# Up projections of both MLPs as pair products, with the halves of the bank added as it is emptied

## The chip, the cores and the metric

The kernel runs on one core of a Trainium2 chip. Its time is the device time of one execution in microseconds; before and after are compared by the median of several executions on the same chip. A profiled execution is recorded as well: every instruction of each engine with its start and duration.

The engines are TensorE (PE in the profile, with its weight loads as PEld), VectorE (DVE), ScalarE (ACT), GpSimd (POOL) and SyncE (SP, which here only issues DMAs). TensorE writes its products into eight banks of 512 float32 columns in each of 128 partitions.

## The reference

A decoder trunk of two layers over a sequence of 256 tokens with 1024 features. The first layer mixes tokens with a gated linear recurrence, the second with sparse attention; behind each mixer stands a squared-ReLU MLP, and the change is in the MLPs alone:

```python
def _sq_relu_mlp(h, w_up, w_down):
    u = jax.nn.relu(h @ w_up)
    return (u * u) @ w_down

def reference(x, ...):
    for i in range(DEPTH):
        h = _rmsnorm(x, norm_mix[i])
        ...
        h = _rmsnorm(x, norm_ffn[i])
        x = x + _sq_relu_mlp(h, mlp_w_up[i], mlp_w_down[i])
    return _rmsnorm(x, norm_final)
```

All inputs are float32. `w_up` is 1024 x 4096 and `w_down` 4096 x 1024, so the up projection of an MLP has 32 chunks of 128 output features.

## The kernel before

**Products in parts.** To come close to float32 with the faster format float32r, each operand is split into a rounded part (high) and the rest (low). A product of weights w and input x is then wh·xh + wh·xl + wl·xh. Two helpers issue this for one step, that is one block of 128 input features:

- `mm3` (L373 to L377) makes three products of 256 columns each, all into the same 256 columns of a bank.
- `mm2` (L379 to L382), the pair, makes two. The first has 512 columns: wh times the high and the low part of x, which lie side by side; it fills both halves of the bank. The second, of 256 columns, adds wl·xh to the lower half. The two halves have to be added later.

**The MLP** (`mlp`, from L832) runs twice. Its input is the tile `hhl` (L549), which holds for each of the KC = 8 feature blocks the high and the low part, 256 columns each, side by side (`hh` and `hl` are views of it). In the up projection a chunk m of 128 output features takes 8 steps, from one weight piece of 128 x 1024. The first chunks (`first`; LEADS = 3 in the first MLP, 4 in the second) have been issued by the section before. The others use `mm3` on the lower half of the next bank from `zrot`, a rotation over six banks. After each chunk `up_post` empties the bank:

- VectorE takes the maximum with 0 and multiplies by `rs`, the factor of the norm (L843), into `t`.
- `flush()` issues what was put off by the chunk before: the low part of the squares (L850).
- `tick` (L344) prepares coming weight pieces: `split_lo` (VectorE, L331) makes the low part of a piece whose high part exists, and `split_hi` (ScalarE, L322) rounds the next one, both only while fewer than LOOK = 6 pieces are ahead. A DMA on SP's queue fills one of NRAW = 5 raw buffers, four pieces ahead of `split_hi`; the split pieces lie in NSPL = 7 pairs of buffers.
- ScalarE squares `t` twice, into `u` in float32 (L848) and rounded into `uh` (L849).

The down projection has 8 chunks of 32 steps. Chunks 0 to 6 use `mm2` on the tiles `uhl`, and chunk 7 uses `mm3`. At the end of a pair chunk ScalarE copies the upper half of the bank into `part` (L876), `residual` adds the lower half to `xt` (L595), and VectorE adds `part` (L879).

Each engine works through its queue in the program's order. In the MLPs that order is the order of the lines; in the sections before them (recurrence, attention and the lead-in chunks) it is worked out when the program is built, by a list scheduler with assumed durations, and is the same in every execution.

Of the kernel before, what the change touches and what calls it, by code (L numbers as in the profile page):

```python
# [12 lines left out]
F32 = mybir.dt.float32  # L13
F32R = mybir.dt.float32r
AF = mybir.ActivationFunctionType
OP = mybir.AluOpType
# [3 lines left out]
P = 128  # L20
S = 256
D = 1024
KC = D // P
# [249 lines left out]
def trunk_kernel(ctx: ExitStack, tc: tile.TileContext, x_in, vec_in, const_in, w2_in, wts, out):  # L273
    nc = tc.nc
    ctx.enter_context(tc.manual_schedule())
    pe, dve, act, pool = nc.tensor, nc.vector, nc.scalar, nc.gpsimd
# [12 lines left out]
    def rotation(*ids):  # L289
        while True:  # L290
            for i in ids:
                yield bank(i)
# [22 lines left out]
    def split_hi(eng=None):  # L315
        i = state["split"]
        if i >= len(order):
            return
        while state["dma"] <= min(i + 4, len(order) - 1):
            issue()  # L320
        n = piece_cols(*order[i])
        (act.copy if eng is None else eng.tensor_copy)(hi_t[i % NSPL][:, :n], raw_t[i % NRAW][:, :n])  # L322
        state["split"] += 1

    def split_lo(eng=None):
        i = state["lo"]
        if i >= state["split"]:
            return
        n = piece_cols(*order[i])
        hi, lo = hi_t[i % NSPL], lo_t[i % NSPL]  # L330
        (eng or dve).tensor_tensor(lo[:, :n], raw_t[i % NRAW][:, :n], hi[:, :n].bitcast(F32), op=OP.subtract)  # L331
        state["lo"] += 1
# [3 lines left out]
    def later(fn):  # L336
        deferred.append(fn)

    def flush():
        todo, deferred[:] = deferred[:], []  # L340
        for fn in todo:
            fn()

    def tick(lo=None, hi=None, n=1):  # L344
        for i in range(max(n, 1)):
            more = n and state["split"] - state["get"] < LOOK
            if more:
                split_lo(lo)
            if i == 0:
                flush()  # L350
            if more:
                split_hi(hi)

    def get(name, idx):
        i = state["get"]
        assert order[i] == (name, idx), (order[i], name, idx)
        state["get"] += 1
        assert state["lo"] > i
        return hi_t[i % NSPL], lo_t[i % NSPL]

    def turn(x):
        return x.rearrange("p (a b) -> p b a", a=2)

    def pairs(z):
        return z.rearrange("p (b a) -> p b a", a=2)

    def nat(z):
        return z.rearrange("p (b a) -> p a b", a=2)

    def two(x):  # L370
        return x.rearrange("p (a b) -> p a b", a=2)

    def mm3(ps, wh, wl, xh, xl, start, stop):  # L373
        ps, xh, xl = pairs(ps), turn(xh), turn(xl)
        pe.matmul(ps, wh, xh, start=start, stop=False)  # L375
        pe.matmul(ps, wh, xl, start=False, stop=False)  # L376
        pe.matmul(ps, wl, xh, start=False, stop=stop)  # L377

    def mm2(z, wh, wl, x, start, stop):  # L379
        xd = x.rearrange("p (i a b) -> p i b a", i=2, a=2)  # L380
        pe.matmul(z.rearrange("p (i b a) -> p i b a", i=2, a=2), wh, xd, start=start, stop=False)  # L381
        pe.matmul(pairs(z[:, :S]), wl, xd[:, 0], start=False, stop=stop)  # L382
# [166 lines left out]
    hhl = hpool.tile([P, KC, 2, S], F32R, name="hhl")  # L549
    hh, hl = hhl[:, :, 0], hhl[:, :, 1]  # L550
    acc = spool.tile([P, S], F32, name="acc")
    rs = spool.tile([P, S], F32, name="rstd")
# [41 lines left out]
    def residual(z, m):  # L594
        dve.tensor_tensor(two(xt[:, m]), two(xt[:, m]), nat(z), op=OP.add)  # L595


    with ExitStack() as ph:
# [41 lines left out]
        for k in range(KC):  # L640
            g = vec[:, V_GM + k:V_GM + k + 1]
            t = 0.6 * k - 3
# [4 lines left out]
                w=[("hh", k)], t=t)  # L647
# [3 lines left out]
        for q in range(4):  # L651
            for i in range(NFINE):
                w = slice(256 * q, 256 * q + 256)
                hi, lo, rw = hi_t[i][:, w], lo_t[i][:, w], raw_t[i][:, w]
                rk = [("raw0", i, q), ("raw", i)]
                t = 1.2 * q + 0.3 * i - 2.9
                add([("dve", 0.2, 0.0), ("act", 0.31, 0.5)], copy(hi, rw), r=rk, w=[("hi0", i, q)], t=t)
                add("dve", 0.34, diff(lo, rw, hi), r=rk + [("hi0", i, q)], w=[("lo0", i, q)],
                    t=t + 0.1)
        for a, b, n in ((0, 2, 2), (0, 1, 1), (4, 6, 2), (4, 5, 1), (0, 4, 1)):  # L660
            add("dve", 0.07 + 0.267 * n, lambda e, a=a, b=b, n=n: e.tensor_tensor(
                x2[:, a:a + n], x2[:, a:a + n], x2[:, b:b + n], op=OP.add), r=[("x2", b + i) for i in range(n)],
                w=[("x2", a + i) for i in range(n)], t=4 + a / 4)
# [44 lines left out]
        def nextbank():  # L708
            zb["n"] += 1
            return (0, 1, 2, 3, 4, 5, 7)[(zb["n"] - 1) % 7]  # L710
# [105 lines left out]
        for m in range(8):  # L816
            wh, wl, wk = sec.weight("out", m, to + 2.65 * m)
            b = nextbank()
            z = sec.bank(("out", m), b, zcols)
# [6 lines left out]
            t = to + 2.65 * (m + 1)  # L826
# [5 lines left out]
    def mlp(layer, epilogue, first, late=None):  # L832
        with ExitStack() as ph:
            up = ph.enter_context(tc.tile_pool(name="up%d" % layer, bufs=1, side="right"))
            tmp = ph.enter_context(tc.tile_pool(name="mtmp%d" % layer, bufs=2))
            uhl = [up.tile([P, 2 * S], F32R, name="uhl", tag="uhl", bufs=NF) for _ in range(NF)]
            uh, ul = [x[:, :S] for x in uhl], [x[:, S:] for x in uhl]
            zrot = rotation(*((LEADS[layer] + i) % 6 for i in range(6)))
            part = [tmp.tile([P, S], F32, name="part", tag="part", bufs=1)]

            def up_post(m, z):
                t = tmp.tile([P, S], F32, name="t", tag="t")
                dve.scalar_tensor_tensor(two(t), nat(z), 0.0, two(rs), op0=OP.max, op1=OP.mult)  # L843
                flush()
                if m >= len(first) - 1:
                    tick(n=2 if m < 16 else 1)
                u = tmp.tile([P, S], F32, name="u", tag="u")
                act.activation(u, t, AF.Square)  # L848
                act.activation(uh[m], t, AF.Square)  # L849
                later(lambda: dve.tensor_tensor(ul[m], u, uh[m].bitcast(F32), op=OP.subtract))  # L850

            for m in range(NF):
                if m >= len(first):
                    z = next(zrot)[:, :S]
                    wh, wl = get("up%d" % layer, m)
                    for k in range(KC):
                        w = slice(k * P, (k + 1) * P)
                        mm3(z, wh[:, w], wl[:, w], hh[:, k], hl[:, k], k == 0, k == KC - 1)
                else:
                    z = first[m]()  # L860
                up_post(m, z)
            for m in range(8):
                z = next(zrot)
                for j in range(4):
                    if j == 3 and late and m == 7:
                        late()
                    wh, wl = get("dn%d" % layer, m * 4 + j)
                    for k in range(8):
                        w, i = slice(k * P, (k + 1) * P), j * 8 + k
                        if m < 7:  # L870
                            mm2(z, wh[:, w], wl[:, w], uhl[i], i == 0, i == NF - 1)
                        else:
                            mm3(z[:, :S], wh[:, w], wl[:, w], uh[i], ul[i], i == 0, i == NF - 1)
                    if j == 3:
                        if m < 7:
                            act.copy(two(part[0]), nat(z[:, S:]))  # L876
                        residual(z[:, :S], m)
                        if m < 7:
                            dve.tensor_tensor(xt[:, m], xt[:, m], part[0], op=OP.add)  # L879
                        epilogue(m)  # L880
                    tick()
# [4 lines left out]

    nc.gpsimd.dma_start(w2raw, w2_in)
    mlp(0, to_mix, up0)


    with ExitStack() as ph:
# [108 lines left out]
        for i in range(2):  # L1000
            pecol = (V_PEK, V_PEV)[i]
            add("pool", 0.15, lambda e, i=i, c=pecol: e.tensor_copy(zf[:, ZW * i + 60], vec[:, c:c + 16]), r=zok + ["vec"],
                w=[("z", i, "p")], t=-5)
# [304 lines left out]
        def out_t(half, m, b, t, step):  # L1308
            wh, wl, wk = weight("o%d" % half, m // 2, t)
            z = zview(("out", half, m), b, zcols)  # L1310
            for ks in ((0, 1), (2, 3)) if half == 0 else ((0, 1), (2,), (3,)):
                def run(e, ks=ks):
                    for kk in ks:
                        o = (m % 2) * 512 + kk * P
                        k = half * 4 + kk
                        mm3(z(), wh[:, o:o + P], wl[:, o:o + P], oh(k), ol(k), kk == 0, kk == 3)
                add("pe", 0.355 * len(ks), run, r=wk + [(n, half * 4 + kk) for n in ("oh", "ol") for kk in ks],
                    w=[("ps", b)], t=t)
                t += step * len(ks) / 2
            add("dve", 0.34, lambda e: residual(z(), m), r=[("ps", b)], w=[("xt", m)], t=t)  # L1320
            return t
# [14 lines left out]
        t, tp_, nb, early = 0.0, {}, 0, True  # L1336
        for x in PROJ:
# [15 lines left out]
            if x == AFTER:  # L1353
                t = max(t, tc_ + TQ)
# [27 lines left out]
        for m in range(8):  # L1382
            t = out_t(1, m, (2, 3, 4, 0, 1)[m % 5], te - 2 + 1.4 * m, PJ)
# [10 lines left out]

    st = bank(6)
    mlp(1, to_final, up1, lambda: square_sums(st, acc, True, False))
    square_sums(st, sqs[1], False, True)
    act.activation(rcol, st[:, :2], AF.Sqrt, bias=epst, scale=1.0 / D)
# [120 lines left out]
```

## Time and profile before

| | us |
|---|---|
| timed executions | 569.47, 569.96, 570.29 (median 569.96) |
| profiled execution | 569.74 |
| its span, first to last instruction | 567.9 |

The span in stages, read from where the lines of each stage start and end: the recurrence and its projections up to about 87 us, the first MLP from there to about 258 us (down projection from 174), attention to about 387 us, the second MLP to about 559 us (down projection from 474), and the last norm. A row of the view of groups names line, engine, operation, output and inputs with their shapes, then the busy time, the mean of one in ns, and the idle time before them with what ended it. A row of the timeline gives start, duration, engine, line and operation, and in brackets the idle time of the engine before it and who ended that. The durations of products overlap, because TensorE takes the next one while the last is still flowing out; the pace is read from the starts.

### The profile page before, as it was taken

What the parts mean: (1) busy time and instruction counts of PE and PEld (TensorE: products, weight loads), DVE (VectorE), ACT (ScalarE), POOL (GpSimd) and SP (SyncE); (2) the same over time, 40 slices, a digit from 0 to 9 for tenths busy, and PEclk for the clock granted to TensorE, in tenths of its full rate; (3) what the DMA queues carried; (4) which work ended last, traced back from release to release, by engine and by line L of the source; (5) the groups of instructions that cost most, each with busy time, mean ns of one, the idle gap of its engine ahead of it and who ended that gap; (6) DMA issues with size and microseconds to landing.
All of it is one profiled execution on the core that took longest, in us unless ns stands there. A gap on an engine that the chain in (4) does not pass through costs nothing.

```text
span 567.9 us, 11331 instructions
## 1 busy us (share of the span) xinstructions
PE 553.5 (97%) x4318; PEld 531.4 (94%) x4318; DVE 429.3 (76%) x884; ACT 370.2 (65%) x738; POOL 51.1 (9%) x63
## 2 busy tenths in 40 slices
PE   8999999999999999999999999998999999999994
PEld 8999999999999999999998997988999999999994
DVE  5999999776775674767999999899876776465532
ACT  6699775766664543546899899996865665354420
POOL 0310000000000211312000101000000000142220
PEclk9999999999999999999999999999999999999997
DMA  8935465655566466566745464542765566556402
GB/s 272 404 139 186 149 221 207 228 199 187 194 211 228 154 216 219 172 189 247 227 149 165 105 171 118 149 94 89 268 217 191 193 209 216 198 176 214 167 1 74
DMA packets 32614, 105.25 MB, mean 185 GB/s; under 512 B 3984, under 2 KB 6944, under 8 KB 32560
## 3 DMA queue, kind: packets, MB, share of 16 engines
q1 hardware_dynamic: 30784, 99.70, 52.5%
q0 software_dynamic: 1200, 4.29, 3.4%
q8 instruction: 34, 0.56, 0.4%
q10 hardware_dynamic: 576, 0.53, 0.3%
q14 instruction: 20, 0.16, 0.1%
HBM read 101.36 MB, written 1.05 MB: 180 GB/s over the span
## 4 chain that ended last, share of the span: by engine, by line
PE 77%; ACT 10%; DVE 8%; issue 2%; DMA 1%; SPq 1%; DVEq 0%; ACTq 0%
PE bank L381 17%; PE bank L375 15%; PE bank L376 15%; PE bank L377 15%; PE bank L382 9%; PE bank L752 2%; ACT pt L1233 2%; ACT pt L1252 2%; ACT whl L388 2%; ACT pth L1266 1%; DMA raw<-in_dram 1%; DVE whl L385 1%; DVE pt L1230 1%; ACT zwoh L388 1%; ACT osum L1299 1%
## 5 line engine op out<-in xcount | busy, mean ns | idle before, releaser
L375 PE MATMUL bank<-hhl,whl 128*128 128x256 f32 x768 | 213.7, 278 | 0.4 <-ACT hhl L643 0.4
L376 PE MATMUL bank<-hhl,whl 128*128 128x256 f32 x768 | 211.5, 275 | 0.1
L377 PE MATMUL bank<-hhl,whl 128*128 128x256 f32 x768 | 211.5, 275 | 0.1
L331 DVE TENSOR_TENSOR whl<-raw,whl 128x1024 fp32r<-128x1024 f32 x117 | 146.0, 1269 | 2.8 <-ACT whl L322 2.8
L375 PEld LDWEIGHTS bank<-hhl,whl 128*128 128x128 f32 x768 | 147.0, 191 | 1.0 <-ACT hhl L643 0.6
L376 PEld LDWEIGHTS bank<-hhl,whl 128*128 128x128 f32 x768 | 147.0, 191 | 0.8 <-DVE hhl L645 0.5
L377 PEld LDWEIGHTS bank<-hhl,whl 128*128 128x128 f32 x768 | 147.0, 191 | 0.4 <-DVE whl L385 0.3
L381 PE MATMUL bank<-uhl,whl 128*128 128x512 f32 x448 | 146.8, 382 | 0.0
L322 ACT CAST whl<-raw 128x1024 fp32r<-128x1024 f32 (+1 forms) x118 | 119.9, 1039 | 9.9 <-ACT whl L322 5.6
L382 PE MATMUL bank<-uhl,whl 128*128 128x256 f32 x448 | 122.1, 273 | 0.0
L381 PEld LDWEIGHTS bank<-uhl,whl 128*128 128x128 f32 x448 | 84.7, 189 | 11.8
L382 PEld LDWEIGHTS bank<-uhl,whl 128*128 128x128 f32 x448 | 86.0, 192 | 0.0
L385 DVE TENSOR_TENSOR whl<-raw,whl 128x1024 fp32r<-128x1024 f32 (+3 forms) x69 | 72.6, 1072 | 0.6 <-ACT whl L388 0.4
L595 DVE TENSOR_TENSOR xt<-xt,bank 128x256 f32<-128x256 f32 x40 | 16.1, 415 | 72.0 <-ACT part L876 58.5
L388 ACT CAST whl<-raw 128x1024 fp32r<-128x1024 f32 (+2 forms) x64 | 60.0, 959 | 6.0 <-DMA raw<-in_dram 4.3
L848 ACT ACTIVATE u<-t 128x256 f32<-128x256 f32 x64 | 26.7, 416 | 53.8 <-DVE t L843 52.5
L843 DVE SCALAR_TENSOR_TENSOR t<-bank,rstd 128x256 f32<-128x256 f32 x64 | 26.9, 423 | 41.5 <-PE bank L377 40.5
L876 ACT COPY part<-bank 128x256 f32<-128x256 f32 x14 | 5.2, 372 | 61.8 <-PE bank L382 61.8
L1233 ACT ACTIVATE pt<-pt,mx 128x128 f32<-128x128 f32 (+1 forms) x64 | 28.6, 450 | 2.1 <-DVE mx L1230 2.1
L850 DVE TENSOR_TENSOR uhl<-u,uhl 128x256 fp32r<-128x256 f32 x64 | 26.6, 416 | 1.8 <-ACT uhl L849 1.7
L565 POOL TENSOR_TENSOR acc<-xt 128x256 f32<-128x256 f32 x2 | 2.9, 1460 | 265.3 <-issue 152.4
L565 POOL TENSOR_TENSOR sq<-xt 128x256 f32<-128x256 f32 x12 | 17.3, 1442 | 94.6 <-DVE xt L879 86.5
(214 smaller groups left out, 871.2 us busy)
## 6 DMA issues: line engine op xcount, KB each, us to landing
raw<-in_dram SPq DMA_DIRECT2D x171, 512.0 KB, 4.4
whl<-in_dram POOLq DMA_DIRECT2D x8, 512.0 KB, 5.7
gw<-in_dram SPq DMA_DIRECT2D x4, 512.0 KB, 9.4
raw<-in_dram SPq DMA_DIRECT2D x5, 256.0 KB, 6.4
xt<-in_dram SPq DMA_DIRECT2D x4, 256.0 KB, 5.6
zwol<-in_dram SPq DMA_DIRECT2D x2, 512.0 KB, 5.4
raw<-in_dram SPq DMA_DIRECT2D x2, 456.0 KB, 3.9
kh<-th SPq DMA_DIRECT2D x8, 64.0 KB, 3.4
```

Source lines behind the costliest of these rows:

```text
L322: (act.copy if eng is None else eng.tensor_copy)(hi_t[i % NSPL][:, :n], raw_t[i % NRAW][:, :n])
L331: (eng or dve).tensor_tensor(lo[:, :n], raw_t[i % NRAW][:, :n], hi[:, :n].bitcast(F32), op=OP.subtract)
L375: pe.matmul(ps, wh, xh, start=start, stop=False)
L376: pe.matmul(ps, wh, xl, start=False, stop=False)
L377: pe.matmul(ps, wl, xh, start=False, stop=stop)
L381: pe.matmul(z.rearrange("p (i b a) -> p i b a", i=2, a=2), wh, xd, start=start, stop=False)
L382: pe.matmul(pairs(z[:, :S]), wl, xd[:, 0], start=False, stop=stop)
L385: return lambda e: e.tensor_tensor(o, a, h.bitcast(F32), op=OP.subtract)
L388: return lambda e: (e.copy if e is act else e.tensor_copy)(o, a)
L843: dve.scalar_tensor_tensor(two(t), nat(z), 0.0, two(rs), op0=OP.max, op1=OP.mult)
L848: act.activation(u, t, AF.Square)
L1233: add("act", (0.39, 0.49)[qc], lambda e, row=row, j=j: e.activation(row, row, AF.Exp, bias=mx[:, j:j + 1], scale=-1.0, accum_out=sm[:, j:j ...
```

## The change

The chunks of the up projections that the MLP issues itself now use `mm2` on the whole bank. In `up_post` such a chunk has ScalarE copy the upper half of the bank into a new tile `b`, then comes the tick (which also flushes), and only then VectorE adds the lower half and `b` into `t` and takes the maximum and the factor in place. The lead-in chunks, which another function issues with `mm3`, are emptied as before.

```diff
             def up_post(m, z):
                 t = tmp.tile([P, S], F32, name="t", tag="t")
-                dve.scalar_tensor_tensor(two(t), nat(z), 0.0, two(rs), op0=OP.max, op1=OP.mult)
-                flush()
+                if m < len(first):
+                    dve.scalar_tensor_tensor(two(t), nat(z), 0.0, two(rs), op0=OP.max, op1=OP.mult)
+                    flush()
+                else:
+                    b = tmp.tile([P, S], F32, name="b", tag="b")
+                    act.copy(two(b), nat(z[:, S:]))
                 if m >= len(first) - 1:
                     tick(n=2 if m < 16 else 1)
+                if m >= len(first):
+                    dve.tensor_tensor(two(t), nat(z[:, :S]), two(b), op=OP.add)
+                    dve.scalar_tensor_tensor(t, t, 0.0, rs, op0=OP.max, op1=OP.mult)
                 u = tmp.tile([P, S], F32, name="u", tag="u")
                 act.activation(u, t, AF.Square)
                 act.activation(uh[m], t, AF.Square)
@@
                 if m >= len(first):
-                    z = next(zrot)[:, :S]
+                    z = next(zrot)
                     wh, wl = get("up%d" % layer, m)
                     for k in range(KC):
                         w = slice(k * P, (k + 1) * P)
-                        mm3(z, wh[:, w], wl[:, w], hh[:, k], hl[:, k], k == 0, k == KC - 1)
+                        mm2(z, wh[:, w], wl[:, w], hhl[:, k].rearrange("p i s -> p (i s)"), k == 0, k == KC - 1)
                 else:
                     z = first[m]()
                 up_post(m, z)
```

## The prediction

> **What bounds the kernel now.** I read the page's table of busy shares and its chain first, because they say which engine the end hangs on.
>
> ```profile
> PE 553.5 (97%) x4318; PEld 531.4 (94%) x4318; DVE 429.3 (76%) x884; ACT 370.2 (65%) x738; POOL 51.1 (9%) x63
> PEclk9999999999999999999999999999999999999997
> PE bank L381 17%; PE bank L375 15%; PE bank L376 15%; PE bank L377 15%; PE bank L382 9%; PE bank L752 2%; ACT pt L1233 2%; ACT pt L1252 2%; ACT whl L388 2%; ACT pth L1266 1%; DMA raw<-in_dram 1%; DVE whl L385 1%; DVE pt L1230 1%; ACT zwoh L388 1%; ACT osum L1299 1%
> ```
>
> TensorE is busy 97% of the span at a granted clock that is full almost throughout, and the chain lies mostly on the products of mm3 (L375 to L377) and mm2 (L381, L382). A busy share of pipelined products doesn't say that they run back to back, so I asked for the stretch in which the change acts (the windows view): 24 chunks of the first up projection, then all pair chunks of the down projection behind it, then its last chunk, which still uses mm3.
>
> ```profile
> 107.03:171.35 64.32, 64.32 (x578) 64.32 (x577) 45.45 (x72) 40.01 (x72) 0.00 (x0) 1.00 0.59 197
> 173.83:247.19 73.36, 73.36 (x450) 67.42 (x449) 45.20 (x49) 32.40 (x41) 13.02 (x11) 1.00 0.61 205
> 247.19:257.91 10.72, 10.72 (x98) 10.72 (x97) 6.68 (x7) 4.67 (x6) 2.32 (x2) 1.00 0.56 183
> ```
>
> The columns are length, PE, PEld, DVE, ACT, POOL, granted clock, DMA share, GB/s. PE has no idle time in any of the three, the clock is 1.00, and in the up stretch VectorE works 45.45 of 64.32 us and ScalarE 40.01. So the pace of the up projections is the pace at which TensorE takes products, and the other engines have about 0.78 us (VectorE) and 1.01 us (ScalarE) of slack in each of the 24 chunks.
>
> **What a step of each form costs.** The ends of these stretches come from the timeline.
>
> ```profile
> 107.03 0.42 DVE L843 SCALAR_TENSOR_TENSOR t<-bank,rstd 128x256 f32<-128x256 f32 x1 [0.79 <-PE bank L377]
> 171.35 0.42 DVE L843 SCALAR_TENSOR_TENSOR t<-bank,rstd 128x256 f32<-128x256 f32 x1 [0.79 <-PE bank L377]
> 173.83 0.38 PE L381 MATMUL bank<-uhl,whl 128*128 128x512 f32 x1
> 174.05 0.27 PE L382 MATMUL bank<-uhl,whl 128*128 128x256 f32 x1
> 174.16 0.38 PE L381 MATMUL bank<-uhl,whl 128*128 128x512 f32 x1
> 247.19 0.28 PE L375 MATMUL bank<-uhl,whl 128*128 128x256 f32 x1
> 257.91 0.28 PE L375 MATMUL bank<-hhl,whl 128*128 128x256 f32 x1
> ```
>
> L843 empties a bank as soon as its chunk is done, so its starts tick with the chunks: 25 of them from 107.03 to 171.35 make 24 chunks in 64.32 us, 2.680 us a chunk and, with 8 steps, **335.0 ns a step of mm3**. The down projection holds 7 chunks of 32 pair steps between 173.83 and 247.19: 73.36 / 224 = **327.5 ns a step of mm2**. Its eighth chunk, on the same input tiles, with mm3, takes 10.72 / 32 = 335.0 ns. Both forms stream 768 columns a step, so the pair saves nothing in columns; it saves one product and one weight load of three, and that is worth 7.5 ns. The eighth chunk is the check that the form is the cause and not the stage.
>
> **Part 1, the products.** The change gives the pair form to 32 - 3 = 29 chunks of the first MLP and 32 - 4 = 28 of the second; the lead-in chunks keep mm3. 57 x 8 = 456 steps x 7.5 ns = **3.42 us** off TensorE. The trace doesn't show a pair with hhl as moving operand. Its bounds are 335.0 ns (nothing gained) and 327.5 ns; I take 327.5, the nearest row, since the width, the weights, the bank rotation and the layout (high part, then low part, in 512 adjacent columns) are those of L381.
>
> That sum can be put beside a rule. The fixed cost per product in these rows: with c for 256 columns and f for a start, 3c + 3f = 335.0 and 3c + 2f = 327.5, so f = 7.5 ns.
>
> The Trainium skill, page "TensorE: Matmul & The Clock Gate", section "Back-to-back issue gap", gives a product of N columns a time of N / 2.4 + 2.5 ns at full clock. By that rule a step would save 2.5 ns and the change an estimated 1.14 us. The trace doesn't agree with it in size: the 335.0 and 327.5 ns above differ by three times as much.
>
> **Part 2, emptying the bank.** Each of the 57 chunks loses one instruction that reads the bank (L843) and gets three: a ScalarE copy of the upper half, a VectorE addition out of the lower half, and the max-and-multiply, now within SBUF. The down projection has the first two already.
>
> ```profile
> 184.20 0.27 PE L382 MATMUL bank<-uhl,whl 128*128 128x256 f32 x1
> 184.51 0.37 ACT L876 COPY part<-bank 128x256 f32<-128x256 f32 x1 [4.30 <-PE bank L382]
> 184.91 0.42 DVE L595 TENSOR_TENSOR xt<-xt,bank 128x256 f32<-128x256 f32 x1 [5.25 <-ACT part L876]
> 185.37 0.42 DVE L879 TENSOR_TENSOR xt<-xt,part 128x256 f32<-128x256 f32 x1
> ```
>
> The copy starts 0.04 us after the chunk's last product (184.20 + 0.27), the addition 0.40 after the copy, and an instruction that needs the addition's result 0.46 after that. The max-and-multiply without a bank is not in the trace; its bounds are the neighbours 0.41 (L850, SBUF only) and 0.42 (L843), so I take 0.42. VectorE gets 57 x 0.42 = 24 us more, ScalarE 57 x 0.37 = 21 us more. Neither is on the path as long as one chunk's work fits in the new chunk of 8 x 327.5 = 2.62 us.
>
> To see whether it fits, one round before:
>
> ```profile
> 131.15 0.42 DVE L843 SCALAR_TENSOR_TENSOR t<-bank,rstd 128x256 f32<-128x256 f32 x1 [0.79 <-PE bank L377]
> 131.49 0.41 DVE L850 TENSOR_TENSOR uhl<-u,uhl 128x256 fp32r<-128x256 f32 x1
> 131.82 1.22 DVE L331 TENSOR_TENSOR whl<-raw,whl 128x1024 fp32r<-128x1024 f32 x1
> 131.67 0.42 ACT L848 ACTIVATE u<-t 128x256 f32<-128x256 f32 x1 [1.02 <-DVE t L843]
> 131.99 0.40 ACT L849 ACTIVATE uhl<-t 128x256 fp32r<-128x256 f32 x1
> 132.30 1.03 ACT L322 CAST whl<-raw 128x1024 fp32r<-128x1024 f32 x1
> ```
>
> By busy times, with the overlaps not taken off, VectorE needs 0.42 + 0.42 + 0.41 + 1.22 = 2.47 us a chunk and ScalarE 0.37 + 0.42 + 0.40 + 1.03 = 2.22, both under 2.62.
>
> **Part 3, the added wait.** The copy now stands at the head of ScalarE's queue until the chunk's last product. Behind it wait the rounding of a coming weight piece (L322) and the two squares. Before, L322 ran ahead of that moment. Who waits for L322 is L331 on VectorE, in the next tick, and the DMA of a later piece. With T for the end of a chunk: copy T + 0.04, L322 0.31 later and done at T + 1.38, addition T + 0.44, max-and-multiply T + 0.90, squares from T + 1.42 (0.52 after it, as 131.15 to 131.67) to T + 2.14. The copy of the next chunk stands ready then, at T + 2.66. On VectorE L331 can start at about T + 1.48, L850 at T + 2.62 (1.14 later, the spacing of such instructions: 1.22 less the overlap of 0.08 seen between L843 and L850), and it leaves the engine free at T + 2.96, just ahead of the next addition at T + 3.06. If that slips, the round that sets the pace is L322, L331, L850, addition, max-and-multiply, square, square, copy, which spans two chunks: 1.03 + 0.10 + 1.14 + 0.34 + 0.46 + 0.52 + 0.32 + 0.31 + 0.31 = 4.53 us, or 2.27 a chunk. So it keeps up.
>
> TensorE itself is further off still. Its weights are split up to six pieces ahead (LOOK), and a bank is used again six chunks later, five chunks or 13.1 us after it was filled; it will be given back at about T + 0.9 us instead of T + 0.45. Cost: nothing, hidden by the stock. At the start of each MLP ScalarE runs some chunks late (0.75 us shorter work than a chunk, so it catches up in a few chunks); the second MLP starts with three pieces in stock and takes two at once there:
>
> ```profile
> 400.93 0.43 DVE L850 TENSOR_TENSOR uhl<-u,uhl 128x256 fp32r<-128x256 f32 x1 [0.18 <-ACT uhl L849]
> 401.87 1.23 DVE L331 TENSOR_TENSOR whl<-raw,whl 128x1024 fp32r<-128x1024 f32 x1 [0.51 <-ACT whl L322]
> 403.01 0.42 DVE L843 SCALAR_TENSOR_TENSOR t<-bank,rstd 128x256 f32<-128x256 f32 x1
> 403.78 2.35 DVE L331 TENSOR_TENSOR whl<-raw,whl 128x1024 fp32r<-128x1024 f32 x2
> 410.38 0.42 DVE L843 SCALAR_TENSOR_TENSOR t<-bank,rstd 128x256 f32<-128x256 f32 x1 [0.64 <-PE bank L377]
> ```
>
> L331 at 401.87 finishes piece 7, which TensorE begins when chunk 6 ends, near 407.7 (chunk 7 ends just before 410.38, less 2.68); the piece has over 4 us to spare, and a delay of one ScalarE copy (0.37) and one addition (0.42) doesn't use that up.
>
> Loads: a 512 KB piece per 2.62 us is 200 GB/s, and the down projection took 205 in the windows view at this very pace. No DMA is added; on SP's queue the load of a piece waits for the raw buffer that L331 frees, and L331 of a tick now stands ahead of the bank's emptying, at T - 1.14 us instead of 131.82, which is T + 0.70, so loads may go earlier, not later. L322 of a tick goes from 1.5 us before T to 0.35 after it; the pieces in stock cover that. The last chunk's low part comes about 1 us later; the down projection reads it at step 31, 10 us on. Cost nothing.
>
> **The sum.** Parts 2 and 3 lie beside TensorE, so what is left is Part 1. Each chunk end moves everything after it, since the attention section's orders are fixed and relative. The profiled execution took 569.74 us (span 567.9 and 1.84 around it); less 3.42 it is 566.32 (span 564.5). The three timed runs have their median, 569.96, 0.22 above the profiled one, so I predict **566.54**, with 1.74 us from the first MLP and 1.68 from the second.
>
> **The rivals.**
> - *Only a small start cost is saved.* The 7.5 ns could belong to the low-part tile of the down projection and not to the form. For it: no row shows a pair with hhl. Against it: the eighth down chunk runs mm3 on the same tiles at 335.0 ns. At a third of the saving, 2.5 ns, 569.96 - 1.14 = 568.82. Chance 3%.
> - *The attention section swallows the first MLP's part.* There VectorE and ScalarE are as full as TensorE:
>
> ```profile
> 280.00:396.00 116.00, 112.28 (x901) 105.61 (x899) 110.77 (x377) 105.56 (x293) 6.40 (x12) 1.00 0.48 132
> ```
>
>   If one of its transfers or backlogs kept to its own time, only the 28 later chunks would count: 569.96 - 1.68 = 568.28. Against it: all of its inputs hang on the first MLP's output or on buffers that come free with it, and nothing there runs by an absolute time. Chance 4%.
> - *The emptying becomes the bound (slower).* Place: the round of Part 3. It decides once a round takes longer than 2.62 us by more than the stock allows: the banks give 13.1 - 0.9 = 12.2 us over 29 chunks, 0.42 each, so above about 3.04 us a chunk. That needs the two-chunk round to close within one chunk, which happens if L331 has to wait for the L322 of its own tick (no piece of lead left). Then 4.53 us a chunk: 566.54 + 57 x (4.53 - 2.62) - 2 x 12.2 = 651. The ticks put L331 ahead of L322, and six pieces lie between, so I give it and anything else that makes the kernel slower 3%.
>
> That the pair form doesn't do what it says can be left out: the down projection runs it.
>
> **How the numbers follow.** Forecast 90%, rivals 3, 4 and 3%. The timed runs spread from 569.47 to 570.29, so the same 3.42 off them gives 566.05 to 566.87. Upwards I allow for a third of the saving lost (1.1 us) to steps slower than 327.5 ns or to late chunks at the start of an MLP: 566.0 to 567.6. About 0.2% (1.1 us) is what a measurement of this kernel can tell from no change. The forecast and the swallowed part are faster by more than that (94%), the small start cost is at the edge and counts as the same (3%), slower 3%.
>
> **What would show it.** Right: in the windows view of an up projection, PE without idle time, 2.62 us from one addition to the next, 456 products and weight loads fewer (about 3862 each), the second MLP's first products 1.74 us earlier and the end 3.4 us earlier. Wrong: idle time of PE in that stretch with a bank or whl as releaser (the third rival), a step of over 330 ns without idle time (the first), or an end of the attention section at the old time (the second).

## The result, and the profile after

| | before | after |
|---|---|---|
| median, us | 569.72 (569.47 to 570.29, 4 runs) | 566.23 (565.92 to 566.76, 4 runs) |
| profiled execution, its span, us | 569.74, 567.9 | 566.76, 565.0 |

The ratio is 0.9938 with a 95% interval from 0.9921 to 0.9956: 3.5 us less, where 3.42 were forecast. The time itself, 566.23, lies 0.3 us from the 566.54 on record. One execution of a kernel further down, the one with the lead-in chunks as pairs too, took 2022.45 us, with every stage between 3.4 and 3.8 times as long; why is not known, and no median or ratio here counts it.

The page of the changed kernel, busy shares and the chain that ended last:

```profile
PE 550.8 (97%) x3862; PEld 516.5 (91%) x3862; DVE 456.7 (81%) x941; ACT 390.8 (69%) x795; POOL 51.2 (9%) x63
PE bank L381 35%; PE bank L382 17%; PE bank L375 6%; PE bank L377 6%; PE bank L376 6%; PE bank L752 2%; ACT pt L1240 2%; DVE whl L385 1%; ACT pt L1259 1%; DVE pt L1237 1%; ACT whl L388 1%; DMA raw<-in_dram 1%; DVE ptl L1274 1%; ACT zwoh L388 1%; ACT pth L1273 1%
```

The products are 456 fewer, as counted, and the chain moved from the lines of mm3 to those of mm2. VectorE has 27 us more work and ScalarE 21 us more, and the chain hardly shows it. The windows view of both changed up projections (columns as before: length, PE, PEld, DVE, ACT, POOL, clock, DMA share, GB/s):

```profile
96.54:172.52 75.98, 75.98 (x466) 69.83 (x465) 70.20 (x119) 59.62 (x119) 0.00 (x0) 1.00 0.63 218
398.14:471.50 73.36, 73.36 (x450) 67.42 (x449) 68.53 (x116) 58.92 (x117) 0.00 (x0) 1.00 0.66 219
```

PE is without a gap in both. 29 chunks of 8 steps in 75.98 us and 28 in 73.36 us are 327.5 ns a step each, the down projection's pace to the tenth of a nanosecond. VectorE is now busy 70.20 of 75.98 us, so the room that was there before is nearly used.

Where the time went, by stage, from the start of the first product of each stage in the timeline (the rows of after below; those of before are at 87.41, 173.83, 257.91, 386.17, 474.50 and, for the last transposes, 561.39):

```profile
87.83 0.28 PE L375 MATMUL bank<-hhl,whl 128*128 128x256 f32 x1
172.52 0.38 PE L381 MATMUL bank<-uhl,whl 128*128 128x512 f32 x1
256.60 0.28 PE L375 MATMUL bank<-hhl,whl 128*128 128x256 f32 x1
384.85 0.28 PE L375 MATMUL bank<-hhl,whl 128*128 128x256 f32 x1
471.50 0.38 PE L381 MATMUL bank<-uhl,whl 128*128 128x512 f32 x1
558.39 0.43 PE L592 MATMUL bank<-cst,rcol 128*128 128x128 f32 x2 [0.55 <-DVE rcol L1406]
```

| stage | before, us | after, us | difference |
|---|---|---|---|
| up to the first lead-in product | 87.41 | 87.83 | +0.42 |
| up projection 1, with lead-in | 86.42 | 84.69 | -1.73 |
| down projection 1 | 84.08 | 84.08 | 0.00 |
| attention | 128.26 | 128.25 | -0.01 |
| up projection 2, with lead-in | 88.33 | 86.65 | -1.68 |
| down projection 2 to the last transposes | 86.89 | 86.89 | 0.00 |

Both up projections give what was worked out for them (1.74 and 1.68), and nothing else moved but the first stage, which the change doesn't touch. It is told below that this stage differs by more than that from one execution to the next; it is why the spans differ by 2.9 and not by 3.4 us.

One round of the emptying in the changed kernel, from the timelines of VectorE and ScalarE:

```profile
130.73 0.42 DVE L857 TENSOR_TENSOR uhl<-u,uhl 128x256 fp32r<-128x256 f32 x1
131.26 0.42 DVE L852 TENSOR_TENSOR t<-bank,b 128x256 f32<-128x256 f32 x1
131.72 0.42 DVE L853 SCALAR_TENSOR_TENSOR t<-t,rstd 128x256 f32<-128x256 f32 x1
132.21 1.23 DVE L331 TENSOR_TENSOR whl<-raw,whl 128x1024 fp32r<-128x1024 f32 x1
130.85 0.37 ACT L848 COPY b<-bank 128x256 f32<-128x256 f32 x1 [0.51 <-PE bank L382]
131.12 1.05 ACT L322 CAST whl<-raw 128x1024 fp32r<-128x1024 f32 x1
132.24 0.42 ACT L855 ACTIVATE u<-t 128x256 f32<-128x256 f32 x1
133.47 0.37 ACT L848 COPY b<-bank 128x256 f32<-128x256 f32 x1 [0.51 <-PE bank L382]
```

Copy to addition 0.41, addition to max-and-factor 0.46, on to the square 0.52: the three spacings that were taken from the down projection and the old round. The copy waits 0.51 us for TensorE in each round, so ScalarE is ahead of it, and the copies tick at 2.62 us (130.85 to 133.47).

### The profile page after: what moved, and what is told of

Its sections match the earlier page's. It is cut to its first block, busy times and chain, and to the rows that moved or that the text cites. A ratio compares the mean times of both kernels' runs of the same rounds, so it can differ in the third digit from the quotient of the medians.

```text
span 565.0 us, 10528 instructions
## 1 busy us (share of the span) xinstructions
PE 550.8 (97%) x3862; PEld 516.5 (91%) x3862; DVE 456.7 (81%) x941; ACT 390.8 (69%) x795; POOL 51.2 (9%) x63
## 4 chain that ended last, share of the span: by engine, by line
PE 77%; DVE 10%; ACT 8%; issue 2%; DMA 2%; SPq 0%; DVEq 0%; ACTq 0%
PE bank L381 35%; PE bank L382 17%; PE bank L375 6%; PE bank L377 6%; PE bank L376 6%; PE bank L752 2%; ACT pt L1240 2%; DVE whl L385 1%; ACT pt L1259 1%; DVE pt L1237 1%; ACT whl L388 1%; DMA raw<-in_dram 1%; DVE ptl L1274 1%; ACT zwoh L388 1%; ACT pth L1273 1%
## 5 line engine op out<-in xcount | busy, mean ns | idle before, releaser
L331 DVE TENSOR_TENSOR whl<-raw,whl 128x1024 fp32r<-128x1024 f32 x117 | 146.5, 1272 | 5.9 <-ACT whl L322 3.1
L381 PE MATMUL bank<-hhl,whl 128*128 128x512 f32 x456 | 149.4, 382 | 0.0
L382 PE MATMUL bank<-hhl,whl 128*128 128x256 f32 x456 | 124.3, 273 | 0.0
L381 PEld LDWEIGHTS bank<-hhl,whl 128*128 128x128 f32 x456 | 86.2, 189 | 12.0
L375 PE MATMUL bank<-hhl,whl 128*128 128x256 f32 x312 | 88.3, 283 | 0.0
L382 PEld LDWEIGHTS bank<-hhl,whl 128*128 128x128 f32 x456 | 87.6, 192 | 0.0
L377 PE MATMUL bank<-hhl,whl 128*128 128x256 f32 x312 | 86.2, 276 | 0.2
L376 PE MATMUL bank<-hhl,whl 128*128 128x256 f32 x312 | 86.1, 276 | 0.1
L377 PEld LDWEIGHTS bank<-hhl,whl 128*128 128x128 f32 x312 | 59.7, 191 | 0.9 <-DVE whl L385 0.8
L376 PEld LDWEIGHTS bank<-hhl,whl 128*128 128x128 f32 x312 | 59.7, 191 | 0.8 <-DVE hhl L645 0.5
L375 PEld LDWEIGHTS bank<-hhl,whl 128*128 128x128 f32 x312 | 59.7, 191 | 0.6 <-issue 0.2
L848 ACT COPY b<-bank 128x256 f32<-128x256 f32 x57 | 21.0, 369 | 21.3 <-PE bank L382 21.2
```

What stands on the lines that cost most here:

```text
L848: act.copy(two(b), nat(z[:, S:]))
```

## The experiments

The theory: TensorE takes products without a gap, a pair step is 7.5 ns shorter, and all that was added to the other engines is hidden. The rivals: the emptying costs something that the gain hides; the attention section swallows a part; and for the gain itself, that it comes from something else than the missing product. The excerpts of the diffs are against the changed kernel, if nothing else is said; `...` stands for lines left out.

### Products alone

The pair products, with the bank emptied as before. The high weights times the low input part lie in the upper half of the bank and are left out of the sum.

```diff
...
-                    b = tmp.tile([P, S], F32, name="b", tag="b")
-                    act.copy(two(b), nat(z[:, S:]))
+                dve.scalar_tensor_tensor(two(t), nat(z[:, :S]), 0.0, two(rs), op0=OP.max, op1=OP.mult)
+                flush()
...
-                    dve.tensor_tensor(two(t), nat(z[:, :S]), two(b), op=OP.add)
-                    dve.scalar_tensor_tensor(t, t, 0.0, rs, op0=OP.max, op1=OP.mult)
```

> This kernel leaves out the product of rounded weights and low input part from the sum (the upper half of the bank is written but not added); it issues the pair products as in the change and empties the bank as before. My theory (TensorE's step sets the pace and the new way of emptying is hidden): same time as the change, about 3.4 us under the kernel before, 2.62 us a chunk, no idle time of PE in the up projections. Rival (the copy, the addition and the wait on ScalarE cost something that the gain hides): faster than the change, by up to the 7.5 ns a step that the up projections could still gain, so more than 3.4 us under the kernel before.

Measured: 566.74 us (566.40 to 567.33), ratio to before 0.9948 (0.9933 to 0.9963). The up projections with their lead-in took 84.69 and 86.65 us, to the hundredth those of the change. The windows view of the first one, from its first pair product to the first down product, has the length of the change's, with less work on VectorE and ScalarE:

```profile
96.51:172.49 75.98, 75.98 (x467) 69.83 (x466) 55.84 (x90) 50.21 (x92) 0.00 (x0) 1.00 0.63 213
```

Taking the added copy and addition away gains nothing.

### Emptying alone

```diff
-                    act.copy(two(b), nat(z[:, S:]))
+                    act.copy(two(b), nat(z))
...
-                    dve.tensor_tensor(two(t), nat(z[:, :S]), two(b), op=OP.add)
+                    dve.tensor_tensor(two(t), nat(z), two(b), op=OP.max)
...
-                        mm2(z, wh[:, w], wl[:, w], hhl[:, k].rearrange("p i s -> p (i s)"), k == 0, k == KC - 1)
+                        mm3(z, wh[:, w], wl[:, w], hh[:, k], hl[:, k], k == 0, k == KC - 1)
```

> Keeps three products a step as before, and empties the bank in the new order: ScalarE copies the columns, VectorE takes the maximum of bank and copy (which changes no value) in the place of the addition, then max and factor. My theory: within 0.3 us of the kernel before, PE without idle time, 2.68 us a chunk. Rival (the emptying costs): slower than before, with idle time of PE in the up projections; with 0.05 us a chunk it would be 2.9 us slower.

Measured: 569.48 us (569.23 to 569.89) beside 569.47 for the kernel before, ratio 0.9996 (0.9986 to 1.0005); the up projections took 86.43 and 88.33 us, before 86.42 and 88.33. The windows view of the same stretch, 29 chunks of 2.68 us with PE busy throughout:

```profile
95.83:173.55 77.72, 77.72 (x699) 77.72 (x697) 70.10 (x119) 59.81 (x119) 0.00 (x0) 1.00 0.64 214
```

The added work costs nothing at this pace, and by the products alone nothing at 2.62 us a chunk either, so the whole gain is TensorE's.

### Same columns, three products

```diff
+    def mm3h(z, wh, wl, xh, xl, start, stop):
+        lo, up, xh, xl = pairs(z[:, :S]), pairs(z[:, S:]), turn(xh), turn(xl)
+        pe.matmul(lo, wh, xh, start=start, stop=False)
+        pe.matmul(up, wh, xl, start=False, stop=False)
+        pe.matmul(lo, wl, xh, start=False, stop=stop)
...
-                        mm2(z, wh[:, w], wl[:, w], hhl[:, k].rearrange("p i s -> p (i s)"), k == 0, k == KC - 1)
+                        mm3h(z, wh[:, w], wl[:, w], hh[:, k], hl[:, k], k == 0, k == KC - 1)
```

> Like the change, but the 512 columns of the first product are issued as two products of 256, the second into the upper half of the bank; same columns, same emptying. My theory (the saving is one product start and one weight load less): 335 ns a step, 2.68 us a chunk, time as before (within 0.3 us). Rival (the saving comes from not adding to columns that were written just ahead): 327.5 ns a step, time as after the change, 3.4 us under the kernel before.

Measured: 569.42 us (569.24 to 570.29), ratio 1.0001 (0.9991 to 1.0010), up projections 86.43 and 88.34 us. With both halves of the bank in use and the new emptying, three products take as long as ever. The gain hangs on issuing two and not on where the sums go.

### The first MLP alone

```diff
-                if m < len(first):
+                if m < len(first) or layer:
                     dve.scalar_tensor_tensor(two(t), nat(z), 0.0, two(rs), op0=OP.max, op1=OP.mult)
...
+                        if layer:
+                            mm3(z, wh[:, w], wl[:, w], hh[:, k], hl[:, k], k == 0, k == KC - 1)
+                        else:
+                            mm2(z, wh[:, w], wl[:, w], hhl[:, k].rearrange("p i s -> p (i s)"), k == 0, k == KC - 1)
```

> The change in the first MLP alone. My theory (each MLP keeps what it gains): 1.74 us under the kernel before, the attention section as long as before to 0.1 us. Rival (the attention section swallows the first MLP's part): within 0.3 us of the kernel before, the attention section up to 1.7 us longer.

Measured: 567.77 us (567.55 to 568.33), 1.70 under the 569.47 beside it, ratio 0.9969 (0.9956 to 0.9981). The first up projection took 84.69 us, attention 128.25, the second up projection 88.34. Attention passes on what it gets.

### What a product costs beside its columns

The prediction read the 7.5 ns as the cost of a product's start, on top of 104.2 ns for 256 columns. Products of half the width test that. Here the kernel before (the edit is shown against it) issues each product of the first MLP's own chunks as two of 128 columns:

```diff
+    def mm6(ps, wh, wl, xh, xl, start, stop):
+        ps, xh, xl = pairs(ps), turn(xh), turn(xl)
+        for i in range(2):
+            pe.matmul(ps[:, i * 64:i * 64 + 64], wh, xh[:, i * 64:i * 64 + 64], start=start and i == 0, stop=False)
...
-                        mm3(z, wh[:, w], wl[:, w], hh[:, k], hl[:, k], k == 0, k == KC - 1)
+                        (mm3 if layer else mm6)(z, wh[:, w], wl[:, w], hh[:, k], hl[:, k], k == 0, k == KC - 1)
```

> The kernel before, with each 256-column product of the first MLP's own up chunks issued as two of 128 columns with the same weights (six products and six weight loads a step instead of three). What a product costs beside its columns: if a start costs 7.5 ns on top of 104.2 ns for 256 columns, a step takes 6 x 59.6 = 358 ns and the up projection is 232 x 0.023 = 5.2 us longer; if it is N / 2.4 + 2.5 ns as the Trainium skill's page TensorE: Matmul & The Clock Gate has it, 335 ns and no change; if each product has to wait for its weight load, and that is what holds a 256-column product at 111.7 ns, 6 x 111.7 = 670 ns and 78 us longer.

Measured in one execution: 647.07 us, 77.7 over the 569.33 beside it. The timeline of PE, pairs of merged products (x2):

```profile
129.78 0.39 PE L387 MATMUL bank<-hhl,whl 128*128 128x128 f32 x2
130.00 0.39 PE L389 MATMUL bank<-hhl,whl 128*128 128x128 f32 x2
130.23 0.39 PE L391 MATMUL bank<-hhl,whl 128*128 128x128 f32 x2
130.45 0.39 PE L387 MATMUL bank<-hhl,whl 128*128 128x128 f32 x2
```

A step of six is 0.67 us (129.78 to 130.45), 111.7 ns a product, what one of 256 columns takes in mm3. The windows view shows PE and PEld both busy without a gap:

```profile
107.00:207.00 100.00, 100.00 (x898) 100.00 (x898) 35.54 (x56) 31.60 (x57) 0.00 (x0) 1.00 0.29 99
```

So in a row of such products 111.7 ns is a floor, and not columns plus a start. Attention in the kernel before shows it at other widths: its products of 122 columns (L1029, from 299.88 to 303.23 us) start 111.7 ns apart too, and rows of products of 304 columns (L1093 to L1095) 129 ns.

The pair doesn't sit on this floor. From start to start its wide product takes 218.5 ns and its narrow one 109.0, as means over the 456 new steps. Three rows of the changed kernel, rounded to 0.01 us:

```profile
96.54 0.38 PE L381 MATMUL bank<-hhl,whl 128*128 128x512 f32 x1
96.76 0.27 PE L382 MATMUL bank<-hhl,whl 128*128 128x256 f32 x1
96.87 0.38 PE L381 MATMUL bank<-hhl,whl 128*128 128x512 f32 x1
```

Both are 0.426 ns a column, and 768 columns at that pace are the 327.5 ns. Three narrow products in a row pay the floor three times, 335.0. The 7.5 ns are therefore not one start that is missing, but three times the 2.5 ns between the floor and 109.2, which is a third of 327.5.

The Trainium skill, page "TensorE: Matmul & The Clock Gate", section "Back-to-back issue gap", gives N / 2.4 + 2.5 ns for N columns, an estimated 215.8 ns for the wide product and 109.2 for the narrow one; the pair's 218.5 and 109.0 lie within 3 ns of that. The same section keeps this rule for isolated products and says that in a stream of loads and products both set the spacing; the 111.7 ns of the narrow rows agree with that. The same page's section "LDWEIGHTS (loading the stationary operand)" gives an estimated 106.7 ns for a load of 128 columns, 5 ns under the floor measured.

For the load as the cause speaks that the weight loads (PEld) have no gap where narrow products follow each other (64.32 of 64.32 us in the up stretch before, 100.00 of 100.00 here) and have gaps beside the pairs (69.83 of 75.98). But the narrow product of the pair has its load too and takes 109.0, and no run changed the loads by themselves, so that the floor is the load's own is argued and not shown.

### How far the emptying is from the bound

One more, then three more VectorE instructions per chunk, which change no value:

```diff
                     dve.scalar_tensor_tensor(t, t, 0.0, rs, op0=OP.max, op1=OP.mult)
+                    for _ in range(3):
+                        dve.tensor_tensor(t, t, t, op=OP.max)
```

> The change with one more VectorE instruction per chunk (t = max(t, t), 128x256, changes no value) between max-and-factor and the squares. While VectorE runs late it takes 2.27 us a chunk after the change (106.23 to 108.50 in its timeline); with 0.45 more it is 2.72, which is 0.10 over TensorE's 2.62. My theory (TensorE only waits once the stock of banks and split pieces, some 12 us, is used up): the backlog grows to about 3 us in an MLP and no time is lost, 566.2 within 0.3 us, PE without idle time. Rival (the emptying stands on the path, so that each added piece counts): 0.10 x 57 = 5.7 us slower than the change, or 26 us if all of it counts.

> The same with three more VectorE instructions per chunk: 2.27 + 3 x 0.45 = 3.62 us a chunk, 1.00 over TensorE's pace. My theory: the backlog passes the stock of 12.2 us after some 12 chunks, then VectorE sets the pace; (29 - 12.2) + (28 - 12.2) = 33 us slower than the change, about 599, PE idle only in the later half of each up projection. Rival (no stock): 57 us slower. Rival (VectorE is never the bound): no loss.

Measured with one: 566.96 us (566.28 to 567.68), ratio to before 0.9958 (0.9943 to 0.9973); up projections 84.68 and 86.66 us, as in the change. Nothing is lost there, though VectorE runs late all the way. The median lies 0.7 us over the change's, more than the 0.3 that was allowed; in the profiled executions the difference is in the first stage alone (first lead-in product at 88.22 us, in the change at 87.83). The backlog is larger than the 3 us expected. The last addition of the first MLP is

```profile
179.43 0.42 DVE L852 TENSOR_TENSOR t<-bank,b 128x256 f32<-128x256 f32 x1
```

6.5 us after the first down product (172.90), while in the change it starts 0.66 us after it (173.18 and 172.52).

Measured with three: 622.03 us (620.74 to 623.86), 56 over the change and not 33. The windows view of the first MLP, up projection and down projection, and rows of PE's waits in the timeline:

```profile
96.88:189.04 92.16, 80.32 (x466) 69.86 (x466) 87.01 (x175) 48.72 (x101) 0.00 (x0) 1.00 0.47 158
189.04:284.28 95.24, 87.21 (x546) 79.34 (x545) 67.49 (x88) 46.40 (x67) 15.37 (x13) 0.98 0.59 195
```
```profile
131.92 0.38 PE L382 MATMUL bank<-hhl,whl 128*128 128x256 f32 x1 [0.55 <-DVE whl L331]
135.56 0.38 PE L382 MATMUL bank<-hhl,whl 128*128 128x256 f32 x1 [0.75 <-DVE whl L331]
201.10 0.38 PE L382 MATMUL bank<-uhl,whl 128*128 128x256 f32 x1 [0.75 <-DVE whl L331]
```

The first up projection took 92.16 us instead of 75.98, 16.2 more, where 16.8 were expected (29 rounds at 1.00 less the stock of 12.2); the second, from the transposes of the norm in its lead-in to the first down product, 91.04 us instead of 75.64, 15.4 more where 15.8 were. So the up projections lose about what was reckoned, but the size of the stock was met in part by luck: it was reckoned from the banks, and what TensorE waits for is the low part of the weights (L331). The last addition of the first MLP's up projection shows how far VectorE was behind; below it two waits of TensorE in the down projection and, from the windows view, the stretch of lower clock at the second of them:

```profile
204.94 0.42 DVE L852 TENSOR_TENSOR t<-bank,b 128x256 f32<-128x256 f32 x1
205.08 0.48 PE L381 MATMUL bank<-uhl,whl 128*128 128x512 f32 x1 [1.96 <-DVE uhl L859]
208.72 0.80 PE L381 MATMUL bank<-uhl,whl 128*128 128x512 f32 x1 [3.05 <-DVE uhl L859]
```
```profile
208.46:211.88 3.42, 3.16 (x10) 2.71 (x11) 3.07 (x5) 2.65 (x4) 0.00 (x0) 0.50 0.64 193
```

The addition starts 15.9 us after the first down product (189.04), in the change 0.66, so the backlog had grown to 15.2 us. The down projections then took 95.24 and 99.0 us instead of 84.08 and 86.9, 11.2 and 12.1 more: the backlog that the stock covered is handed on, and TensorE waits there for the weight pieces and the last squares (the rows at 205.08 and 208.72). A smaller part is the clock: with the wait of 3.05 us the granted clock fell to 0.50, for 3.4 us in the first down projection (the windows row) and 6.8 us in the second, and a pair step took 0.64 us there instead of 0.33. These slow steps cost 1.6 and 2.6 us of the 11.2 and 12.1. The stock lends time; it doesn't give it.

### Going on in the same direction

First the seven lead-in chunks as pairs too, emptied like the others and run twice, then the last down chunk of the first MLP in addition:

```diff
+            wide = name[:2] == "up"
-            z = self.bank((name, idx), b, zcols)
+            z = self.bank((name, idx), b, (lambda x: x) if wide else zcols)
...
+                        if wide:
+                            mm2(z(), wh[:, w], wl[:, w], hhl[:, k].rearrange("p i s -> p (i s)"), k == 0, k == KC - 1)
```

> The change, and the seven lead-in chunks of the two MLPs as pairs as well, emptied in the same way. My theory (a step of a pair saves 7.5 ns wherever TensorE sets the pace): 56 x 7.5 ns = 0.42 us less than the change, 0.18 us before the first norm's transposes and the rest after them. Rival (at the start of an MLP the emptying is late already, so the added copies count, or the scheduled part around the lead-in loses its fit): no gain, or a loss of up to 1 us.

> The same kernel as e8, for its profile: the change and the seven lead-in chunks as pairs. My theory: 0.42 us under the change, 24 lead-in steps of the first MLP and 32 of the second at 327.5 ns instead of 335.0, all other stages unchanged. Rival: the stages around the lead-in longer by as much.

Measured: 565.86 us (565.80 to 566.25, three executions), ratio 0.9940 (0.9924 to 0.9957), and 565.86 us (565.78 to 567.25, four), ratio 0.9938 (0.9925 to 0.9952), which can't be told from the change. The stages are read from the second run. By stage the first up projection with lead-in is 0.18 us shorter than the change's (84.51), as expected, the second only 0.05 (86.60) where 0.24 were. There TensorE waits at the norm, and it waits longer when it comes earlier: beside the wait that the change has too, one for the sum of squares appears in its timeline,

```profile
392.91 0.61 PE L591 MATMUL bank<-ones,acc 128*128 128x1 f32 x4 [0.15 <-DVE acc L534]
396.39 0.43 PE L596 MATMUL bank<-cst,rcol 128*128 128x128 f32 x2 [1.46 <-DVE rcol L510]
```

where the change has 1.43 at the second and no wait at the first.

```diff
-                        if m < 7:
+                        if m < 7 or not layer:
```

> The change, the seven lead-in chunks as pairs, and the last down chunk of the first MLP as a pair too, emptied like the other seven. My theory (each step that becomes a pair saves one weight load of three: 335.0 to 327.5 ns wherever TensorE sets the pace): 56 x 7.5 ns = 0.42 us in the lead-in chunks, 32 x 7.5 ns = 0.24 us in the last down chunk (10.72 to 10.48 us), together 0.66 us under the change, with the attention section as long as before. Rival (the later emptying of the last down chunk, a copy and an addition more, delays the norm before attention): the attention section longer by up to 0.9 us, which takes back more than the 0.24 us.

Measured: 566.81 us (566.49 to 566.92), ratio 0.9947 (0.9933 to 0.9960). The down projection is 0.24 us shorter (83.84) and attention 0.88 us longer (129.13): the rival's price to the tenth. The timeline of ScalarE and VectorE at the end of that chunk:

```profile
256.20 0.37 ACT L884 COPY part<-bank 128x256 f32<-128x256 f32 x1 [4.41 <-PE bank L382]
256.61 0.42 DVE L599 TENSOR_TENSOR xt<-xt,bank 128x256 f32<-128x256 f32 x1 [3.76 <-ACT part L884]
257.06 0.42 DVE L887 TENSOR_TENSOR xt<-xt,part 128x256 f32<-128x256 f32 x1
```

The next section starts from this sum, and a copy and one more addition stand in front of it, 0.41 and 0.45 us from start to start. A pair pays only where nobody waits for its chunk. Of the versions run, none is measurably better than the change.

## Why the prediction was right

- **What bounds the kernel.** TensorE's pace in the up projections, shown by the emptying alone (no change) and the products alone (all of it).
- **Part 1, 456 steps at 7.5 ns.** Measured 1.73 and 1.68 us for 1.74 and 1.68. The nearest row, the pair of the down projection, was the right one to take, and its lower bound was met exactly. The reading of the 7.5 ns beside it, a start that costs 7.5 on top of 104.2 ns, fell: half as wide a product takes the same 111.7 ns, and the pair's two products take 218.5 and 109.0 where that reading gives 215.8 and 111.7. The sum didn't use it. The Trainium skill's rule beside the sum there (page "TensorE: Matmul & The Clock Gate", section "Back-to-back issue gap") came out at a third of the saving because it counts columns and a start; by the trace, three narrow products in a row sit on a floor above that.
- **Part 2, the emptying.** VectorE got 27 us more where 24 were reckoned, ScalarE 21 for 21. Hidden, as forecast.
- **Part 3, the wait at the head of ScalarE's queue.** The order of a round came as worked out, with L331 at 1.36 us after the copy (1.44 worked out). The late rounds at the start of each MLP run at 2.27 us, the figure of the two-chunk path, but that is chance: it was ScalarE that was to run late, and what holds these rounds is VectorE's own queue, whose four instructions start 0.34, 0.45, 0.34 and 1.14 us after one another.
- **Rivals.** The small start cost: out, by 327.5 ns on hhl tiles. Attention swallowing a part: out, by the first MLP alone. The emptying as bound: it did not occur, and the three added instructions show its mechanism, but the prediction's point of decision, 3.04 us a round, took the stock of 12.2 us for a gift. The down projections lose 11 to 12 us more behind it, so with backlogs that large a slower round costs nearly all of its excess. One added instruction, 2.72 us a round and a last addition 5.9 us later than in the change, cost nothing.
- **Size and spread.** 3.5 us by medians, 3.41 by the two up stages. The span differs by 2.9 because in the profiled execution of after the first lead-in product came 0.42 us later; that arises in the first 19 us, where VectorE and ScalarE wait for the first inputs to land. That the time itself was met to 0.3 us is in part luck: kernels with the same stage lengths from the lead-in on, the products alone and the one added instruction, have medians of 566.74 and 566.96.

## What to carry to other kernels

Compare forms of the same sum by the interval of their steps in the trace of the same kernel, and not by columns: here three products of 256 columns and a pair of 512 and 256 stream the same columns, and the three narrow ones sit on a floor of 111.7 ns each. Before adding work beside a bound engine, add up one round of each other engine in queue order against the new pace, and ask who has to pay a backlog back at the end of the stage. A form that must be gathered afterwards belongs in chunks that nobody is waiting for; in the last chunk before a norm it cost nearly four times what it saved (0.88 us for 0.24).

## What the runs showed of the hardware

- Products in a row, each with its weight load, started 111.7 ns apart at 256, 128 and 122 columns; in the pair the wide product took 218.5 ns and the narrow one 109.0, 0.426 ns a column in both.
- With a wait of 3.05 us of TensorE (three added instructions) the granted clock fell to 0.50 for 3.4 us, and for 6.8 us in the second MLP; a pair step took 0.64 us there and 0.33 elsewhere.
- The first stage, in which the program waits for its inputs, is the least repeatable: the first lead-in product started between 86.96 and 88.54 us in eleven profiled executions of kernels that don't differ in that stage, while attention took 128.21 to 128.29 us in the nine in which it started in the same way. Differences of a few tenths of a microsecond can be read from stages, but not from the time of single executions.
